# A two-layer hybrid decoder trunk: the order of instructions made by the scheduler's timeline model instead of its default one

## Chip, cores and metric

The kernel runs on one core of a Trainium2 chip. The metric is the device time of one execution in microseconds (us); the median of several runs is compared. A core has five engines with a queue of instructions each: TensorE (PE; its weight loads are listed apart as PEld), VectorE (DVE), ScalarE (ACT), GpSimd (POOL) and SyncE (SP), which issues the loads here.

## The reference

Two layers on one sequence of 512 tokens and 2048 channels, all in float32:

```python
for l in range(DEPTH):                               # 2
    h = rms_norm(x, pre_norm_g[l])
    proj = jnp.einsum('bsd,de->bse', h, w_in[l])     # 2048 -> 6656
    (rq, rk, rv, rg, dq, dk, dv, dg, lx, lg) = jnp.split(proj, split_idx, axis=-1)
    ret_out  = rms_norm(retention(rq, rk, rv, positions)) * silu(rg)             # 6 heads x 128, rope, chunks of 128
    diff_out = rms_norm(diff_attention(dq, dk, dv, positions, lam), subln_g) \
               * (1 - lam_init) * silu(dg)                                       # 4 heads, two softmaxes each, rope, causal
    lru_out  = rg_lru(lx, ...) * silu(lg)                                        # 768 channels, conv of 4, block gates, scan
    y = jnp.einsum('bse,ed->bsd', concat([ret_out, diff_out, lru_out]), w_out[l])
    x = x + rms_norm(y, post_norm_g[l])
```

(The reshapes into heads are left out.)

## The kernel before

Both projections are done in passes. A pass makes 512 output columns: four PSUM banks (`big`, 128 x 512 each, four buffers in all), or two in each of the last two passes of a layer. For each bank it runs over 16 blocks of 128 input rows. Every float32 operand is split into a rounded part and a remainder, so one product is three matmuls (`whi` with `hhi`, `whi` with `hlo`, `wlo` with `hhi`); these are the lines L208. With the output projection the second operand is `mhi`/`mlo`. Form "A" has the weights as the stationary operand (queries, keys, LRU inputs), form "B" the activations (values, gates, output).

Weights come in chunks of two row blocks: SP loads `raw`, ACT rounds it to `whi` (L163), DVE subtracts to get `wlo` (L164). There are three buffers of each (`WBUFS = 3`). The matmuls of one chunk for all banks need its `whi` from the first and its `wlo` from the third on.

The passes of a layer follow in this order: values of the differential attention (`dv`), its queries and keys (`dq`, `dk`), three passes for the LRU (`lx`, `lg`), three for the retention's queries and keys (`rq`, `rk`), three for its values and gates (`rv`, `rg`), the attention's gate (`dg`), then the output projection. When a bank is full it is evacuated: for queries and keys L439 makes `qk` on DVE, and the rope follows: two 64-row products on DVE (L399, L400, output `rt2`), two steps on POOL (L401, L406). For values and gates L535, L738, L740 and L742 read the bank.

Between the matmuls of the passes lies the side work, written as generators that are advanced one step for every two bank groups (`pump`): the attention by blocks of 128 queries and heads, the LRU in two halves, the retention by heads, and the norms. One attention unit makes two score tiles `sc` on PE (L462, L463), adds the mask and takes the row maximum `mx` on DVE (L465, L468), exponentiates to `pr` on ACT (L471), combines the two on DVE (L475 to L477), transposes to `wT` on PE (L485, copied by L487), and multiplies by the values into `acc` (L495). The tiles `sc`, `wT` and `hT` share three PSUM buffers (`pm`). A retention head makes `rs` (L661), `rk` (L665), `kv` and `ro` (L686, L689) on PE; its norm is L692 on ACT, L694 and L695 on DVE, L697 on POOL, L698 and L700 on DVE. At the end of a layer's output passes each bank gives `y` (L767 to L797), and `hT` (L805) transposes it for the next layer, where L812 on ACT and L813 on DVE make `hhi` and `hlo` of it in turn. In the output projection the attention's output is transposed by L552 to `dT` and split by L554 (ACT, `mhi`) and L555 (DVE, `mlo`).

The program's text is not the order in which the engines run. The tile framework collects the instructions and orders those of PE, DVE, ACT and POOL itself, among what the data and the buffers allow, and puts in the semaphores; loads and splits of weights and the evacuation of a full bank are given a higher priority in the text. Only SP keeps the order as written:

```python
    ctx.enter_context(tc.manual_schedule(engines={mybir.EngineType.SP}))
...
        for n, (c, b) in enumerate(order):
            ensure(base + max(c, n // nb) + 2)
            mm(c, b)
            if n % 2 == 1:
                pump()
```

Each engine then runs its instructions strictly in that order. In what follows a name such as `wlo_699` is a tile with the number that the program gives it, which is the same before and after; the profile's rows leave the numbers out.

## Time and profile before

| | |
|---|---|
| median of 3 runs | 1665.82 us (1663.75 to 1666.63) |
| the profiled execution | 1666.37 us, span 1664.4 us, mean granted clock 0.993 |
| PE busy | 1634.2 us, 98% of the span |
| DVE, ACT, POOL busy | 928.7, 626.0, 259.1 us |
| HBM read, written | 167.86 MB, 8.39 MB |

The profile is one execution. The span runs from the first to the last instruction. A row of the timeline gives start, length, engine, line, operation, out<-in and, in brackets, how long the engine had been idle before it and what it waited for. A group row gives the count, busy us and mean ns of one, then the idle time before the group and what ended it. The recorded 0.39 us of a matmul overlaps the next one's, so its price is read from the distance of starts. A half clock of TensorE shows as a granted clock near 0.50 in a stretch.

### The profile page before, as it was taken

To read this page: it belongs to the slowest core of one execution; us is meant where nothing else is said; L and a number is where in the kernel's file an instruction comes from. 1 tells how busy PE (TensorE), PEld (TensorE's weight loads), DVE (VectorE), ACT (ScalarE), POOL (GpSimd) and SP (SyncE) were. 2 spreads that over 40 slices of the span, in tenths; PEclk is the share of its full clock that TensorE was granted. 3 is DMA by queue.
4 is the path that set the end of the run, shared out by engine and by line. 5 is a ranking of instruction groups with operands and counts; after the bars stand their busy time and mean duration, and the time that the engine had idled before them with its cause. 6 is when DMAs were issued, how large, how long until landed. Compare 5 with 4: busy or idle time off the path is not lost. (4 is left out here: it accounts for less than half of the span.)

```text
span 1664.4 us, 19440 instructions
## 1 busy us (share of the span) xinstructions
PE 1634.2 (98%) x7541; PEld 1349.5 (81%) x7541; DVE 928.7 (56%) x1474; ACT 626.0 (38%) x966; POOL 259.1 (16%) x216
## 2 busy tenths in 40 slices
PE   9999899999999999999999998999999999999997
PEld 7788788787877888888888887888888888888886
DVE  6767765665674444322772776664677544442336
ACT  6232345457212323222662224346541222332233
POOL 0011400111261110000110131003035301100003
PEclk9999999999999999999999999999999999999999
DMA  7233222232322222344643222222323322223635
GB/s 258 79 92 101 89 64 84 89 96 76 102 76 77 76 89 83 107 146 158 222 159 100 89 89 77 76 84 83 92 86 102 101 73 77 91 96 108 196 124 199
DMA packets 54747, 177.50 MB, mean 107 GB/s; under 512 B 6656, under 2 KB 7680, under 8 KB 54656
## 3 DMA queue, kind: packets, MB, share of 16 engines
q1 hardware_dynamic: 52592, 169.94, 32.2%
q0 software_dynamic: 1920, 6.29, 1.0%
q8 instruction: 59, 0.97, 0.2%
q14 instruction: 32, 0.26, 0.1%
q10 hardware_dynamic: 144, 0.04, 0.0%
HBM read 167.86 MB, written 8.39 MB: 106 GB/s over the span
## 5 line engine op out<-in xcount | busy, mean ns | idle before, releaser
L164 DVE TENSOR_TENSOR wlo<-raw,whi 128x1024 fp32r<-128x1024 f32 (+1 forms) x289 | 370.5, 1286 | 426.7 <-ACT whi L163 412.8
L163 ACT CAST whi<-raw 128x1024 fp32r<-128x1024 f32 (+1 forms) x289 | 302.6, 1049 | 630.2 <-PE big L208 549.1
L208 PE MATMUL big<-hhi,whi 128*128 128x512 f32 x1024 | 402.9, 394 | 1.5 <-DVE lx L635 1.5
L208 PE MATMUL big<-hhi,wlo 128*128 128x512 f32 x1024 | 400.6, 391 | 1.6 <-DVE wlo L164 1.6
L208 PE MATMUL big<-hlo,whi 128*128 128x512 f32 x1024 | 400.0, 391 | 0.0
L208 PE MATMUL big<-whi,hhi 128*128 128x512 f32 x640 | 255.3, 401 | 3.7 <-ACT rv L738 2.6
L208 PE MATMUL big<-wlo,hhi 128*128 128x512 f32 x640 | 252.0, 395 | 2.7 <-DVE wlo L164 2.7
L208 PE MATMUL big<-whi,hlo 128*128 128x512 f32 x640 | 251.6, 393 | 0.0
L208 PEld LDWEIGHTS big<-hhi,wlo 128*128 128x128 f32 x1024 | 192.9, 188 | 42.5 <-DVE wlo L164 2.0
L208 PEld LDWEIGHTS big<-hhi,whi 128*128 128x128 f32 x1024 | 193.0, 188 | 41.7 <-DVE lx L635 2.0
L208 PEld LDWEIGHTS big<-hlo,whi 128*128 128x128 f32 x1024 | 193.0, 189 | 38.8
L208 PE MATMUL big<-wlo,mhi 128*128 128x512 f32 x512 | 199.5, 390 | 0.6 <-DVE wlo L164 0.6
L208 PE MATMUL big<-whi,mlo 128*128 128x512 f32 x512 | 199.8, 390 | 0.0
L208 PE MATMUL big<-whi,mhi 128*128 128x512 f32 x512 | 199.8, 390 | 0.0
L208 PEld LDWEIGHTS big<-wlo,hhi 128*128 128x128 f32 x640 | 121.5, 190 | 29.4 <-DVE wlo L164 3.1
L208 PEld LDWEIGHTS big<-whi,hhi 128*128 128x128 f32 x640 | 121.5, 190 | 28.3 <-ACT rv L738 3.0
L208 PEld LDWEIGHTS big<-whi,hlo 128*128 128x128 f32 x640 | 121.6, 190 | 24.2
L208 PEld LDWEIGHTS big<-wlo,mhi 128*128 128x128 f32 x512 | 96.1, 188 | 21.2 <-DVE wlo L164 1.5
L208 PEld LDWEIGHTS big<-whi,mlo 128*128 128x128 f32 x512 | 96.2, 188 | 19.7
L208 PEld LDWEIGHTS big<-whi,mhi 128*128 128x128 f32 x512 | 96.1, 188 | 19.6
L773 POOL TENSOR_TENSOR ry<-sy,mhalf 128x1 f32<-128x1 f32 x8 | 4.7, 585 | 406.7 <-DVE sy L771 406.7
L471 ACT ACTIVATE pr<-sc,mx 128x128 f32<-128x128 f32 (+3 forms) x64 | 33.3, 525 | 75.7 <-DVE mx L468 75.6
(212 smaller groups left out, 1530.0 us busy)
## 6 DMA issues: line engine op xcount, KB each, us to landing
raw<-in_w_in SPq DMA_DIRECT2D x207, 512.0 KB, 3.6
raw<-in_w_out SPq DMA_DIRECT2D x80, 512.0 KB, 3.5
xT<-in_xt SPq DMA_DIRECT2D x16, 256.0 KB, 6.6
xr<-in_x SPq DMA_DIRECT2D x16, 256.0 KB, 5.5
xs<-y POOLq DMA_DIRECT2D x16, 256.0 KB, 3.5
xr<-xs SPq DMA_DIRECT2D x16, 256.0 KB, 5.5
pg<-in_postg SPq DMA_DIRECT2D x8, 256.0 KB, 3.9
out<-y POOLq DMA_DIRECT2D x8, 256.0 KB, 4.5
```

Of the source, the lines that this page charges most:

```text
L163: last_copy[0] = A.copy(hi[:, a:b, :], raw[:, a:b, :])
L164: V.tensor_tensor(lo[:, a:b, :], raw[:, a:b, :], hi[:, a:b, :], op=ALU.subtract)
L208: T.matmul(ps[b], lhsT=lhsT, rhs=rhs, start=(cnt[b] == 0), stop=(cnt[b] == total - 1))
L471: A.activation(p[:, :n], sc[c][:, :n], AF.Exp, bias=mx[:, c:c + 1], scale=0.125, accum_out=sums[:, h:h + 1])
L773: G.tensor_tensor(st["ry"][tb], ms, mhalf[:, :1], op=ALU.pow)
```

## The change

One argument is added where the kernel is built:

```diff
-    with tile.TileContext(nc) as tc:
+    with tile.TileContext(nc, schedule_with_timeline_sim=True) as tc:
         tile_hybrid_trunk(tc, *args)
```

With it the framework orders PE, DVE, ACT and POOL by a model of when each instruction would run, instead of its default one. The instructions stay the same, except that ACT's activation tables are loaded 27 times instead of 32. SP's order is the same. Three places show how the rows move.

VectorE, keys of the retention in layer 1 (`qk_692` is the last bank of a pass, `wlo_699` the remainder of the next weights, `rt2` the rope halves). The difference between the two orders, first the head of the block, then its end:

```order
 L164 TENSOR_TENSOR wlo_686_3601<-raw_684_3599,whi_685_3600 128x1024
 L439 TENSOR_TENSOR qk_692_3663<-big_647_3363,rsb_99_457 128x512
-L164 TENSOR_TENSOR wlo_699_3671<-raw_697_3669,whi_698_3670 128x1024
 L399 TENSOR_TENSOR rt2_700_3687<-qk_573_2984,sin_r_92 64x512
 L400 TENSOR_TENSOR rt2_700_3687<-qk_573_2984,sin_r_92 64x512
```

```order
 L399 TENSOR_TENSOR rt2_720_3862<-qk_687_3611,sin_r_92 64x512
 L400 TENSOR_TENSOR rt2_720_3862<-qk_687_3611,sin_r_92 64x512
+L164 TENSOR_TENSOR wlo_699_3671<-raw_697_3669,whi_698_3670 128x1024
+L164 TENSOR_TENSOR wlo_703_3706<-raw_701_3704,whi_702_3705 128x1024
 L164 TENSOR_TENSOR wlo_707_3741<-raw_705_3739,whi_706_3740 128x1024
 L164 TENSOR_TENSOR wlo_711_3776<-raw_709_3774,whi_710_3775 128x1024
```

`wlo_699` has moved from just behind `qk_692` to behind all twelve rope halves, and `wlo_703` from among them to just after it.

TensorE, attention of layer 1, from one unit's scores (`sc_375`) on. Before:

```order
L208 MATMUL big_269_1591<-hhi_51_217,wlo_340_1840 128x512
L462 MATMUL sc_375_1995<-st_241_1430,st_205_1188 128x384
L463 MATMUL sc_375_1995<-kl_243_1436,st_205_1188 128x384
L462 MATMUL sc_376_1998<-st_242_1431,st_206_1189 128x384
L463 MATMUL sc_376_1998<-kl_244_1437,st_206_1189 128x384
L485 MATMUL wT_380_2012<-cmt_81,pr_366_1949 128x128 x3
L495 MATMUL acc_349_1879<-dv_109_513,wT_370_1960 128x128
L495 MATMUL acc_349_1879<-dv_110_527,wT_370_1960 128x128
L208 MATMUL big_270_1592<-hhi_48_211,whi_339_1839 128x512
L208 MATMUL big_270_1592<-hlo_49_212,whi_339_1839 128x512
L208 MATMUL big_270_1592<-hhi_48_211,wlo_340_1840 128x512
L208 MATMUL big_270_1592<-hhi_51_217,whi_339_1839 128x512
```

Now:

```order
L462 MATMUL sc_375_1995<-st_241_1430,st_205_1188 128x384
L463 MATMUL sc_375_1995<-kl_243_1436,st_205_1188 128x384
L462 MATMUL sc_376_1998<-st_242_1431,st_206_1189 128x384
L463 MATMUL sc_376_1998<-kl_244_1437,st_206_1189 128x384
L495 MATMUL acc_349_1879<-dv_109_513,wT_370_1960 128x128
L495 MATMUL acc_349_1879<-dv_110_527,wT_370_1960 128x128
L485 MATMUL wT_380_2012<-cmt_81,pr_366_1949 128x128 x3
L462 MATMUL sc_396_2075<-st_249_1491,st_211_1243 128x384
L463 MATMUL sc_396_2075<-kl_251_1497,st_211_1243 128x384
L462 MATMUL sc_397_2078<-st_250_1492,st_212_1244 128x384
L463 MATMUL sc_397_2078<-kl_252_1498,st_212_1244 128x384
L208 MATMUL big_417_2177<-hhi_7_129,whi_389_2049 128x512
```

The big matmuls that stood between the scores and transposes of the units are now ahead of them all; the first big matmul of the next pass (`big_417`) comes right after the third unit's scores (`sc_396`, `sc_397`).

TensorE, retention of layer 2, behind the last output product of head `ro_1861`. Before:

```order
L686 MATMUL ro_1861_10398<-rv_1799_10026,sT_1854_10356 128x128
L689 MATMUL ro_1861_10398<-rst_1860_10382,qk_1665_9154 128x128
L208 MATMUL big_1800_10076<-whi_1845_10300,hhi_1117_6209 128x512
L208 MATMUL big_1800_10076<-whi_1845_10300,hlo_1118_6210 128x512
L208 MATMUL big_1800_10076<-wlo_1846_10301,hhi_1117_6209 128x512
```

Now:

```order
L686 MATMUL ro_1861_10398<-rv_1799_10026,sT_1854_10356 128x128
L689 MATMUL ro_1861_10398<-rst_1860_10382,qk_1665_9154 128x128
L661 MATMUL rs_1887_10526<-qk_1710_9431,qk_1760_9766 128x128 x2
L665 MATMUL rk_1888_10531<-cmt_81,qk_1760_9766 128x128 x3
L208 MATMUL big_1880_10504<-whi_1867_10417,hhi_1087_6095 128x512
L208 MATMUL big_1880_10504<-whi_1867_10417,hlo_1088_6096 128x512
L208 MATMUL big_1880_10504<-wlo_1868_10418,hhi_1087_6095 128x512
```

The new bank `big_1880` takes the buffer of `big_1800`; where the matmuls of `big_1800` to `big_1803` followed the head's output, the next head's `rs` and `rk` and the new bank now do.

## Prediction

> **What bounds the kernel now.** I read the head of the profile page first, then the chain that ended last, then TensorE's waits, then the timeline around the longest waits, and last a table of stretches with the clock.

> ```profile
> span 1664.4 us, 19440 instructions
> PE 1634.2 (98%) x7541; PEld 1349.5 (81%) x7541; DVE 928.7 (56%) x1474; ACT 626.0 (38%) x966; POOL 259.1 (16%) x216
> ```

> TensorE is the bound: 98% busy, while VectorE, the next, stands at 56%. The chain view (start, length, what) gives the price of one matmul:

> ```profile
> 1483.09 147.82 PE big L208 x652
> ```

> 147.82 / 652 = 0.2267 us. The kernel has 6528 of these 128x512 matmuls (17 passes of 16 x 4 x 3 in each of two layers; the diff leaves the count alone), so 1480 us are theirs whatever the order, and the small matmuls of the three mixers fill nearly all the rest. An order can only change how long TensorE stands still. That is the view of waits (total us, times, longest), the larger rows:

> ```profile
> PE sc L462 <- ACT pr L471: 5.2, 3, 2.8
> PE big L208 <- DVE wlo L164: 4.9, 4, 2.7
> PE big L208 <- ACT rv L738: 2.6, 1, 2.6
> PE big L208 <- DVE lx L635: 1.5, 1, 1.5
> PE ssx L915 <- DVE xsq L907: 1.4, 1, 1.4
> PE big L208 <- ACT whi L163: 1.1, 1, 1.1
> ```

> These are 16.7 us; the smaller rows (all under 1 us each, without the start's) bring it to about 20. Four of them in the timeline, with the wait in brackets:

> ```profile
> 199.59 0.33 PE L462 MATMUL sc<-st,st 128*128 128x128 f32 x1 [1.73 <-ACT pr L471]
> 475.59 0.50 PE L208 MATMUL big<-wlo,hhi 128*128 128x512 f32 x1 [2.70 <-DVE wlo L164]
> 505.46 0.50 PE L208 MATMUL big<-whi,hhi 128*128 128x512 f32 x1 [2.59 <-ACT rv L738]
> 1005.05 0.39 PE L462 MATMUL sc<-st,st 128*128 128x128 f32 x1 [2.80 <-ACT pr L471]
> ```

> and behind the three longest, and behind the one at 48.8 us (ssx), the clock is halved. Columns: stretch, its length, busy time of PE, PEld, DVE, ACT, POOL, then granted clock, DMA share, GB/s:

> ```profile
> 49.40:56.30 6.90, 6.90 (x25) 5.79 (x26) 2.17 (x9) 1.29 (x2) 1.03 (x1) 0.51 0.01 2
> 476.10:479.50 3.40, 3.40 (x9) 2.63 (x9) 3.40 (x2) 0.00 (x0) 2.71 (x2) 0.50 0.66 182
> 506.80:510.20 3.40, 3.40 (x10) 2.63 (x9) 1.23 (x1) 1.04 (x1) 0.00 (x0) 0.51 0.28 104
> 1005.20:1012.00 6.80, 6.12 (x17) 4.80 (x18) 3.14 (x12) 2.05 (x8) 0.00 (x0) 0.50 0.43 142
> ```

> A stretch costs half its length: 3.4 + 1.7 + 1.7 + 3.4 = 10.2 us. The wait of 1.73 at 199.6 brought none.

> **What the change removes.** In the new order I followed each waiting instruction back to what it waits for: nearly every wait above has its producer earlier or its reader later. For instance the last weights (wlo) are now read some 14 matmuls before the end, not 24. So 20 us of waits go, 10.2 us of half clock, and 0.1 us at each of about 20 restarts: 32 us. What is late instead are the places below; the rest of the order moves work that keeps its lead, and I set it at nothing because each reader stands at least as many matmuls behind its producer as the producer's chain takes. Where that cover is too short it is in the list.

> **E, retention's keys in layer 1.** VectorE now runs twelve rope halves (L399, L400) between qk_692 and wlo_699; before, wlo_699 came first. In the same place of the trace (rows of VectorE, then groups in the stretch 453.5 to 473.5):

> ```profile
> 445.28 0.69 DVE L439 TENSOR_TENSOR qk<-big,rsb 128x512 f32<-128x512 f32 x1 [0.61 <-PE big L208]
> 448.00 0.69 DVE L439 TENSOR_TENSOR qk<-big,rsb 128x512 f32<-128x512 f32 x1 [2.03 <-PE big L208]
> 451.36 0.69 DVE L439 TENSOR_TENSOR qk<-big,rsb 128x512 f32<-128x512 f32 x1
> L400 DVE TENSOR_TENSOR rt<-qk,sin_r 64x512 f32<-64x512 f32 x6 | 9.1, 1516 | 0.1
> L399 DVE TENSOR_TENSOR rt<-qk,sin_r 64x512 f32<-64x512 f32 x6 | 8.0, 1340 | 0.2
> L164 DVE TENSOR_TENSOR wlo<-raw,whi 128x1024 fp32r<-128x1024 f32 x3 | 6.1, 2028 | 0.1
> ```

> The banks come 2.72 us apart (12 matmuls), so the third, qk_692's, was complete near 450.7. The new order has 56 matmuls from there to the first reader of wlo_699: 56 x 0.2267 = 12.7, so it is wanted at 463.4. VectorE has it at 452.05 + 17.1 + 0.3 of gaps + about 2.0 = 471.4. TensorE stands 8.0 us; such a wait is past any that the trace shows, so I take the longer half-clock stretch, 3.3. **11.3.** From below the ends are 0 (see the rival on ropes), from above 14.

> **RQ and RK, the same in layer 2.** Ten ropes stand ahead of wlo_1733, whose reader comes 74 matmuls (16.8 us) after the last bank; eight stand ahead of wlo_1769 (54 matmuls, 12.2 us). Groups of the stretch 1239.8 to 1255.2:

> ```profile
> L400 DVE TENSOR_TENSOR rt<-qk,sin_r 64x512 f32<-64x512 f32 x5 | 7.4, 1484 | 0.1
> L399 DVE TENSOR_TENSOR rt<-qk,sin_r 64x512 f32<-64x512 f32 x5 | 5.4, 1078 | 0.1
> ```

> Ten are 12.8 us, behind two splits of the mixer rows (1.3) that stay where they were; with 2 us for wlo_1733 it ends 1.5 us late. Eight, at E's means, are 11.4; with wlo 13.4 after qk_1762, whose 0.7 lies past its bank: 2.0 late, 0.5 for clock. **1.5 + 2.5.**

> **C, D: differential attention.** One unit is two score products, a mask and maximum each (L465), L468, two exponentials (L471), the combination (L477), transposes. Groups by line and shape, mean ns in the second number:

> ```profile
> L465 DVE CUSTOM_DVE_ANT_0 sc<-sc,cmt 128x384 f32<-128x384 f32 x16 | 8.7, 572 | 1.8 <-PE sc L463 1.8
> L465 DVE DVE_READ_ACCUMULATOR2_ANT mx<- 128x1 f32 x64 | 9.0, 140 | 0.0
> L471 ACT ACTIVATE pr<-sc,mx 128x384 f32<-128x384 f32 x16 | 9.2, 578 | 22.7 <-DVE mx L468 22.6
> L471 ACT ACTIVATION_READ_ACCUMULATOR pr<-sc,mx 128x1 f32 x64 | 12.5, 196 | 0.0
> L477 DVE SCALAR_TENSOR_TENSOR pr<-pr,cc,pr 128x384 f32<-128x384 f32 x8 | 5.6, 704 | 0.2
> L812 ACT ACTIVATE hhi<-hT,pp 128x128 fp32r<-128x128 f32 x64 | 20.5, 370 | 6.3 <-DVE hlo L813 5.1 <-PE hT L805 1.0
> L813 DVE SCALAR_TENSOR_TENSOR hlo<-hT,pp,hhi 128x128 fp32r<-128x128 f32 x64 | 19.6, 345 | 2.7 <-ACT hhi L812 2.4
> ```

> At C (layer 1, the end of a pass) three units now follow each other on TensorE with no big matmul between. From the scores of sc_365 to pr_366, which wT_380 reads: two L465 1.42, the weight split wlo_423 queued among them 1.3, L468, L475, L476 some 0.5, two exponentials 1.55, the next unit's L465 0.71, L477 0.70: 6.2 us, and a second split (wlo_393) up to 1.3 ahead of it. TensorE has 1.3 us of its own there. 6.1 and 1.7 of clock: **7.8** (2 to 9). At D (layer 2) the same happens once, with wlo_1530 between L465 and L468 of the unit whose pr_1484 is next: waits 3.1, clock 1.7, some 0.2 at the place of the old 2.80: **5.0** (2 to 6).

> **H, layer boundary.** Four hT transposes (1116, 1125, 1158, 1159) now stand in a row with three PSUM buffers for them. One buffer is free after four L812 and four L813 that follow each other by turns: about 4 x 0.37 + 0.35 = 1.8 us, while the post-norm's VectorE work lies between them. Walked by hand: 4.15 us in several waits, and 1.7 of clock: **5.8** (1.5 to 7.5).

> **J, retention in layer 2.** big_1880 now stands directly behind ro_1861, rs_1887 and rk_1888, some 1.0 us of work. It needs the bank of big_1800, which is read by the silu, value and gate instructions queued behind ro_1861's normalisation:

> ```profile
> 1370.18 0.60 ACT L692 ACTIVATE rsq<-ro 128x512 f32<-128x512 f32 x1 [0.74 <-PE ro L689]
> 1370.80 1.28 ACT L535 ACT_TABLE_LOAD   x1
> 1374.61 0.61 DVE L742 SCALAR_TENSOR_TENSOR rg<-big,rstd,rgs 128x128 f32<-128x128 f32 x2 [0.44 <-ACT rv L738]
> ```

> From 1370.1 to 1375.2 are 5.1 us; less 1.0 it waits 4.1, and 1.7 of clock: **5.8** (3 to 7.5). Five of the 32 table loads (1.28 each) vanish from ACT, none of them here; ACT has idle time around them, so I give nothing for that.

> **G, output projection, both layers.** dT_931 and dT_1997 move to just ahead of the first matmul that reads whi_940 (whi_2006). ACT makes that weight after dT's evacuation:

> ```profile
> 663.36 0.69 ACT L554 ACTIVATE mhi<-dT,subg 128x512 fp32r<-128x512 f32 x1 [0.48 <-PE dT L552]
> 663.95 1.04 ACT L163 CAST whi<-raw 128x1024 fp32r<-128x1024 f32 x1
> ```

> 0.69 + 1.04 = 1.7 us in each layer, 3.5, with 0.5 for clock: **4.0** (3.4 to 7). **I**, the LRU gate of layer 1 waiting behind POOL: **1** (0 to 2.5).

> **K, the end.** The last two banks now end 4 matmuls (0.9 us) apart, not 18 (4.1):

> ```profile
> 1655.12 0.39 PE L208 MATMUL big<-wlo,mhi 128*128 128x512 f32 x1
> 1655.60 0.60 ACT L767 ACTIVATE junk<-big 128x512 f32<-128x512 f32 x1 [1.86 <-PE big L208]
> 1657.14 3.08 DVE L797 SCALAR_TENSOR_TENSOR y<-y,ry,xr 128x512 f32<-128x512 f32 x3
> ```

> VectorE's part for a bank is 4 us (three L797, 3.08, and what leads to them). Before, the first bank's ran beside TensorE; now about 3 us of it come between the last matmul and the last outputs: **3** (1 to 4).

> **Sum.** 11.3 + 4.0 + 7.8 + 5.0 + 5.8 + 5.8 + 4.0 + 1 + 3 = 47.7 lost, 32 won: +15.7 on the profiled execution, whose time is 1666.37 (2.0 outside its span). The median of the runs is 0.5 lower, so I say 1681.

> [...] The rows above put the half clock behind waits of 2.6 to 2.8 us. [...]

> **Rivals.** No change: the rope halves at E, RQ and RK take 0.69 us, as some single ones do in the trace, not the mean of 1.4, because POOL's part of the rope falls elsewhere. Then wlo_699 is ready at 452.05 + 8.3 + 1.3 = 461.7, ahead of 463.4, and all three terms go: -15.3, so 1666. For it: RQ's five L399 have a mean of 1078 ns and E's six 1340, so the slow-down depends on what runs beside them. Against: POOL does its part of a rope as soon as these same rope halves let it, so it runs beside the next ones. Faster: every wait of the new order stays below 1.9 us, as most of the old did, so that no half clock follows. Ten places at 1.9 are 19 us against 32: -13, so 1653. It decides from 3 us for a place downwards. For it: only three old waits behind attention and weights were longer; against it: the queues at E, C and J hold 5 to 17 us in rows. Much slower: each of six long waits (C, D, E, H, J, RK) is followed by 6.8 us of half clock, as at 1005, which is up to 10 us more: 1691.

> **How the numbers follow.** My forecast has 0.54, much slower 0.14, no change 0.13, faster 0.19. A change under 0.2% (3.3 us) can't be told from none. Slower 0.68, same 0.13, faster 0.19. The range goes from 1661, below which lies more than half of the faster case, to 1693, above which I leave 0.05; the likeliest case alone has 1673 to 1689.

> **What would show it.** TensorE's waits should show wlo (L164) as the largest releaser, with one of about 8 us near 465 to 475; three waits around sc or wT near 235 to 245 us; one of 4 us behind rg (L742) in the second layer's retention; whi (L163) at both output projections; half clock behind each wait over 2.5 us; and none at 49, 506 and 1005. I am wrong if the waits of TensorE sum to under 25 us, or if VectorE's ropes at E are short.

## The result, and the profile after

The changed kernel takes 1681.28 us (median of 4 runs, 1679.88 to 1683.64) against 1665.38 us for the kernel before on the same chip (1663.75 to 1666.63): a ratio of 1.0097, 95% interval 1.0080 to 1.0115, so 15.9 us slower. The profiled execution took 1679.92 us, 13.6 us more than that of before, with a span of 1678.1 us.

The head of the page after:

```profile
span 1678.1 us, 19433 instructions
PE 1632.7 (97%) x7541; PEld 1350.2 (80%) x7541; DVE 937.0 (56%) x1474; ACT 618.9 (37%) x961; POOL 264.0 (16%) x216
```

TensorE's busy time is 1.5 us less than before and its span 13.7 us more. It does the same work and stands still longer. Its waits by releaser (total us, times, longest), without two rows of 1.4 us (at the start) and 1.2 us:

```profile
PE big L208 <- DVE wlo L164: 13.1, 5, 7.7
PE sc L462 <- ACT pr L471: 5.0, 3, 2.4
PE big L208 <- ACT rgs L535: 4.4, 1, 4.4
PE big L208 <- ACT whi L163: 3.5, 2, 1.8
PE big L208 <- DVE qk L439: 2.5, 1, 2.5
PE hT L805 <- DVE hlo L813: 1.8, 2, 1.5
```

Before, the last weights (`wlo`) were the second entry with 4.9 us; now they are the first with 13.1. The waits of over 1 us one by one, in the timeline, wait in brackets:

```profile
174.81 0.50 PE L208 MATMUL big<-hhi,wlo 128*128 128x512 f32 x1 [1.39 <-DVE wlo L164]
238.31 0.69 PE L462 MATMUL sc<-st,st 128*128 128x384 f32 x1 [2.39 <-ACT pr L471]
307.15 0.50 PE L208 MATMUL big<-hhi,whi 128*128 128x512 f32 x1 [1.23 <-DVE lg L640]
355.35 0.50 PE L208 MATMUL big<-hhi,whi 128*128 128x512 f32 x1 [2.54 <-DVE qk L439]
468.10 0.80 PE L208 MATMUL big<-wlo,hhi 128*128 128x512 f32 x1 [7.70 <-DVE wlo L164]
671.12 0.50 PE L208 MATMUL big<-whi,mhi 128*128 128x512 f32 x1 [1.77 <-ACT whi L163]
849.27 0.66 PE L805 MATMUL hT<-cmt,y 128*128 128x128 f32 x4 [1.49 <-DVE hlo L813]
1083.02 0.50 PE L462 MATMUL sc<-st,st 128*128 128x512 f32 x1 [2.09 <-ACT pr L471]
1252.58 0.50 PE L208 MATMUL big<-hhi,wlo 128*128 128x512 f32 x1 [1.28 <-DVE wlo L164]
1294.30 0.50 PE L208 MATMUL big<-wlo,hhi 128*128 128x512 f32 x1 [2.41 <-DVE wlo L164]
1389.31 0.76 PE L208 MATMUL big<-whi,hhi 128*128 128x512 f32 x1 [4.44 <-ACT rgs L535]
1502.65 0.50 PE L208 MATMUL big<-whi,mhi 128*128 128x512 f32 x1 [1.77 <-ACT whi L163]
```

Only the rows at 174.8 and 355.4 are not in the prediction's list. Stretches of the trace with the granted clock (the third number from the end), first at the three old places near 49, 506 and 1005 us, then at the new ones:

```profile
48.00:56.00 8.00, 8.00 (x38) 6.40 (x37) 5.25 (x12) 4.30 (x6) 0.00 (x0) 1.00 0.20 67
500.00:512.00 12.00, 12.00 (x60) 10.08 (x59) 7.83 (x11) 5.24 (x10) 6.86 (x5) 1.00 0.28 87
1005.00:1012.00 7.00, 7.00 (x34) 5.78 (x33) 4.27 (x15) 3.76 (x11) 0.00 (x0) 1.00 0.52 152
238.00:241.40 3.40, 3.09 (x11) 2.65 (x11) 2.39 (x9) 1.26 (x6) 0.00 (x0) 0.52 0.52 167
463.30:473.50 10.20, 5.40 (x13) 4.25 (x14) 9.10 (x6) 0.00 (x0) 9.90 (x5) 0.51 0.32 101
1084.40:1087.80 3.40, 3.40 (x10) 2.62 (x9) 3.30 (x13) 0.31 (x2) 1.01 (x1) 0.50 0.64 202
1388.20:1395.00 6.80, 5.69 (x14) 4.46 (x15) 3.61 (x12) 2.78 (x8) 2.51 (x2) 0.50 0.02 8
```

The old half-clock stretches are gone, and C, E, D and J of the prediction have one each. (Both kernels have one more behind the last matmul, from 1660.5 us before and from 1671.5 us now, where TensorE has nothing left to do.) Where part of a stretch lies inside the wait it costs nothing: at E TensorE works again from 468.1, so (473.4 - 468.1) / 2 = 2.65 us are lost.

### The profile page after: what moved, and what is told of

Read it like the earlier page. It is cut to its first block, busy times and chain, and to the rows that moved or that the text cites. A ratio compares the mean times of both kernels' runs of the same rounds, so it can differ in the third digit from the quotient of the medians.

```text
span 1678.1 us, 19433 instructions
## 1 busy us (share of the span) xinstructions
PE 1632.7 (97%) x7541; PEld 1350.2 (80%) x7541; DVE 937.0 (56%) x1474; ACT 618.9 (37%) x961; POOL 264.0 (16%) x216
## 4 chain that ended last, share of the span: by engine, by line
PE 90%; DVE 6%; ACT 2%; issue 1%; POOL 0%; DVEq 0%; ACTq 0%; POOLq 0%
PE big L208 82%; DVE wlo L164 1%; PE gate L599 1%; PE acc L495 1%; DVE rt L404 1%; PE ro L686 1%; DVE rt L400 1%; PE rs L661 1%; PE sc L462 1%; PE sc L463 1%; PE ro L689 0%; PE kv L675 0%; PE wT L485 0%; ACT whi L163 0%; PE hT L805 0%
## 5 line engine op out<-in xcount | busy, mean ns | idle before, releaser
L164 DVE TENSOR_TENSOR wlo<-raw,whi 128x1024 fp32r<-128x1024 f32 (+1 forms) x289 | 368.9, 1281 | 428.5 <-ACT whi L163 412.6
L163 ACT CAST whi<-raw 128x1024 fp32r<-128x1024 f32 (+1 forms) x289 | 302.2, 1049 | 614.3 <-PE big L208 530.6
L208 PE MATMUL big<-hhi,whi 128*128 128x512 f32 x1024 | 401.5, 392 | 3.8 <-DVE qk L439 2.5
L208 PE MATMUL big<-hlo,whi 128*128 128x512 f32 x1024 | 400.6, 391 | 0.0
L208 PE MATMUL big<-hhi,wlo 128*128 128x512 f32 x1024 | 394.9, 391 | 3.1 <-DVE wlo L164 3.0
L208 PE MATMUL big<-wlo,hhi 128*128 128x512 f32 x640 | 247.9, 396 | 10.1 <-DVE wlo L164 10.1
L208 PE MATMUL big<-whi,hhi 128*128 128x512 f32 x640 | 251.0, 399 | 4.5 <-ACT rgs L535 4.4
L208 PE MATMUL big<-whi,hlo 128*128 128x512 f32 x640 | 251.2, 394 | 0.0
L208 PEld LDWEIGHTS big<-hhi,wlo 128*128 128x128 f32 x1024 | 192.7, 188 | 45.1 <-DVE wlo L164 4.8
L208 PEld LDWEIGHTS big<-hhi,whi 128*128 128x128 f32 x1024 | 192.7, 188 | 44.9 <-DVE qk L439 3.0
L208 PEld LDWEIGHTS big<-hlo,whi 128*128 128x128 f32 x1024 | 192.7, 188 | 39.2
L208 PE MATMUL big<-whi,mhi 128*128 128x512 f32 x512 | 200.2, 391 | 3.5 <-ACT whi L163 3.5
L208 PE MATMUL big<-whi,mlo 128*128 128x512 f32 x512 | 199.4, 390 | 0.0
L208 PE MATMUL big<-wlo,mhi 128*128 128x512 f32 x512 | 192.1, 389 | 0.0
L208 PEld LDWEIGHTS big<-wlo,hhi 128*128 128x128 f32 x640 | 121.6, 190 | 36.6 <-DVE wlo L164 11.2
L208 PEld LDWEIGHTS big<-whi,hhi 128*128 128x128 f32 x640 | 121.4, 190 | 30.2 <-ACT rgs L535 4.7
L208 PEld LDWEIGHTS big<-whi,hlo 128*128 128x128 f32 x640 | 121.4, 190 | 24.5 <-DVE hlo L813 0.3
L208 PEld LDWEIGHTS big<-whi,mhi 128*128 128x128 f32 x512 | 96.1, 188 | 23.6 <-ACT whi L163 4.0
L208 PEld LDWEIGHTS big<-wlo,mhi 128*128 128x128 f32 x512 | 96.0, 188 | 19.9
L208 PEld LDWEIGHTS big<-whi,mlo 128*128 128x128 f32 x512 | 96.1, 188 | 19.7
L471 ACT ACTIVATE pr<-sc,mx 128x128 f32<-128x128 f32 (+3 forms) x64 | 33.2, 524 | 81.1 <-DVE mx L468 81.1
```

Source lines behind the costliest of these rows:

```text
L163: last_copy[0] = A.copy(hi[:, a:b, :], raw[:, a:b, :])
L164: V.tensor_tensor(lo[:, a:b, :], raw[:, a:b, :], hi[:, a:b, :], op=ALU.subtract)
L208: T.matmul(ps[b], lhsT=lhsT, rhs=rhs, start=(cnt[b] == 0), stop=(cnt[b] == total - 1))
L471: A.activation(p[:, :n], sc[c][:, :n], AF.Exp, bias=mx[:, c:c + 1], scale=0.125, accum_out=sums[:, h:h + 1])
```

## The experiments

The theory: a few places in the new order each put one instruction behind work that outlasts its reader's cover, each costs what its wait and the clock behind it cost, and the costs add. The general rival: the order as a whole sets the time, and a place undone turns up as a wait somewhere else. All edits set the order of issue alone, within one engine's queue; only `pool_late` makes one engine wait for another (with `Sync` in place of `NoSync`). They stand behind the call that writes the program, in this form, and in the diffs below only the pairs are shown (an instruction, the one that it must now follow, and a comment with the tiles):

```diff
         tile_hybrid_trunk(tc, *args)
+        ins = {i.name: i for i in nc.cur_bb.bb.instructions}
+        for later, earlier in (
...
+        ):
+            tc.add_manual_dep(ins[later], earlier, mybir.DependencyInfo(
+                mybir.DependencyClass.NoSync, mybir.DependencyReason.DATA), reason="order")
```

**e_only: place E put back, in the changed kernel.**

```diff
+            ("I-3688", "I-3674"),  # DVE: rope halves rt2_700 behind wlo_699
+            ("I-3689", "I-3674"),  # DVE: rope halves rt2_700 behind wlo_699
+            ("I-3828", "I-3709"),  # DVE: rope halves rt2_716 behind wlo_703
+            ("I-3829", "I-3709"),  # DVE: rope halves rt2_716 behind wlo_703
+            ("I-3863", "I-3744"),  # DVE: rope halves rt2_720 behind wlo_707
+            ("I-3864", "I-3744"),  # DVE: rope halves rt2_720 behind wlo_707
```

> The new order with one place put back: on VectorE wlo_699 stands ahead of the twelve rope halves again, wlo_703 behind eight of them and wlo_707 behind ten; all else as in the new order. Theory (the place in the queue makes the wait): the wait of 7.7 us at wlo_699 and the half clock behind it go, together 10.5 us by the trace after, and no other wait comes: 1681.3 - 10.5 = about 1671. Rival (backlog: VectorE has the same work before the same readers, so the wait only moves to wlo_703 or wlo_707, as before the change, when 2.7 us and 1.7 us of half clock stood there): 1675 or more, with a wait of 2 to 4 us within 10 us of the old one.

Measured: 1672.87 us (1672.67 to 1672.94), ratio 1.0048 (1.0033 to 1.0063), 8.4 us off the changed kernel. The waits behind `wlo`:

```profile
PE big L208 <- DVE wlo L164: 5.4, 4, 2.4
```

7.7 of the 13.1 us are gone, and no other entry grew by more than 0.7. So half of the net loss comes from one place on one engine. The gain is 2 us less than expected. Outside E and ahead of the last matmul the clock was halved for 20.5 us in this profile and for 13.7 in the changed kernel's, and half of the difference, 3.4 us, is lost time; the last section has what was measured of that.

**before_e: the same place, the other way, in the kernel before.**

```diff
+            ("I-3674", "I-3864"),  # DVE: wlo_699 behind the last rope half, rt2_720
+            ("I-3674", "I-3863"),  # DVE: and its first part
```

> The kernel before with this one place of the change made alone: wlo_699 (and with it wlo_703) behind all twelve rope halves on VectorE; nothing else moves. Theory: the first reader of wlo_699 stands 50 matmuls behind the bank, so it is wanted at about 462.0 us and ready at 471.5: a wait of 9 us or a little more, with some 2.5 us of half clock behind it, while the old wait of 2.7 us for wlo_707 and its 1.7 us of half clock vanish, since TensorE then comes later: +7, 1672 to 1674. Rival (the wait is TensorE's standing cost there in any order): within 2 us of 1665.4. If the two costs add instead of replacing each other: 1677.

Measured: 1672.42 us (1671.01 to 1674.04), ratio 1.0042 (1.0026 to 1.0059), +7.4. Its timeline and the stretch of half clock around it:

```profile
473.94 0.79 PE L208 MATMUL big<-wlo,hhi 128*128 128x512 f32 x1 [10.94 <-DVE wlo L164]
```

```profile
466.40:480.10 13.70, 6.16 (x15) 4.81 (x16) 11.83 (x7) 0.00 (x0) 10.61 (x6) 0.50 0.26 86
```

The wait of 2.70 at 475.6, which the kernel before had there, is gone. So the place in VectorE's queue is enough to make the wait, without anything else of the new order. (POOL works here too, for 10.61 us of this stretch; the next run is about that.)

**pool_late: are the ropes long because POOL works beside them?** POOL's first step of seven ropes (L401) waits until VectorE has done the last rope half; VectorE's order stays that of the changed kernel.

```diff
+            ("I-3649", "I-3864"),  # POOL: L401 of qk_571 behind the last rope half on VectorE, L400 rt2_720
+            ("I-3690", "I-3864"),  # POOL: L401 of qk_573 likewise
...
+            ("I-3865", "I-3864"),  # POOL: L401 of qk_687 likewise
```

> The new order, wlo_699 still behind the twelve rope halves, but POOL's first rope steps (L401) of these ropes wait until VectorE has done the last half. Theory (the size of the wait is VectorE running beside POOL): each rope half takes 0.69 us instead of the 1.4 on the mean, the twelve take 8.4 instead of 16.7 us, wlo_699 is ready 8 us earlier, near the time it is wanted: the wait falls from 7.7 to under 1 us and the time to about 1671. Rival (rope halves are slow for another reason, such as the weight splits' or ScalarE's traffic): the halves stay at 1.4 us and the time at 1681.

Measured: 1671.85 us (1670.81 to 1673.23), ratio 1.0042 (1.0027 to 1.0057), 9.4 us off the changed kernel. VectorE's groups at E, first of the changed kernel (449 to 466 us), then of this one (446 to 473 us; count, busy us, mean ns):

```profile
L400 DVE TENSOR_TENSOR rt<-qk,sin_r 64x512 f32<-64x512 f32 x6 | 10.1, 1676 | 0.1
L399 DVE TENSOR_TENSOR rt<-qk,sin_r 64x512 f32<-64x512 f32 x6 | 6.4, 1073 | 0.2
```

```profile
L400 DVE TENSOR_TENSOR rt<-qk,sin_r 64x512 f32<-64x512 f32 x7 | 4.8, 686 | 0.1
L399 DVE TENSOR_TENSOR rt<-qk,sin_r 64x512 f32<-64x512 f32 x7 | 4.8, 686 | 0.1
```

With POOL idle (29.1 us ahead of its L401) each rope half takes 0.686 us, where the means are 1.676 and 1.073 us with POOL at work beside them (14.9 of the 17 us), and the 7.7 us wait goes although `wlo_699` still stands behind all twelve. So two things make E together: the place in the queue, and POOL's work beside it. Either one taken away takes the wait. The prediction's rival "no change" had the right mechanism but not its condition. What in POOL's work lengthens a rope half was not shown.

**j_only, g_only, k_only: three more places put back, each alone.**

```diff
+            ("I-10474", "I-10405"),  # PE: big_1802 from whi_1857 on behind the last product of ro_1861
+            ("I-10486", "I-10405"),  # PE: big_1803 from whi_1845 on likewise
+            ("I-10468", "I-10381"),  # PE: big_1802 from whi_1845 on behind kv_1859
+            ("I-10432", "I-10441"),  # ACT: whi_1870 behind rgs_1872
+            ("I-10433", "I-10449"),  # DVE: wlo_1871 behind rg_1876
+            ("I-10512", "I-10445"),  # ACT: whi_1885 behind rv_1874
```

> The new order with the retention place of layer 2 put back: 18 matmuls of big_1802 and big_1803 stand behind ro_1861 again and cover its normalisation, and ScalarE and VectorE round the next weights behind the evacuation of big_1800. Theory: the chain of 5.1 us behind ro_1861 is covered by 4.1 us of matmuls and some 0.5 us of small ones, so the wait of 4.6 us at big_1880 falls to 0.5 to 1 and its half clock (2.5 us of loss) goes: -6.5, about 1675. Rival (the bank's release is set by something else, such as the table load or the next weights): the wait stays above 3 us and the time above 1679.

Measured: 1676.80 us (1675.25 to 1678.43), ratio 1.0072 (1.0057 to 1.0087), 4.5 us won, 2 us less than expected; this profile has half clock at H and RK, where the changed kernel's has none. What is left of the wait of 4.44 at the first matmul of `big_1880`:

```profile
1390.42 0.47 PE L208 MATMUL big<-whi,hhi 128*128 128x512 f32 x1 [0.76 <-DVE rg L742]
```

```diff
+            ("I-5162", "I-5103"),  # PE: big_937, big_938 from whi_916 on behind dT_931
+            ("I-5168", "I-5103"),  # PE: big_937, big_938 from whi_916 on behind dT_931
+            ("I-11264", "I-11205"),  # PE: big_2003, big_2004 from whi_1982 on behind dT_1997
+            ("I-11270", "I-11205"),  # PE: big_2003, big_2004 from whi_1982 on behind dT_1997
```

> The new order with dT_931 and dT_1997 moved twelve big matmuls ahead of the first reader of whi_940 and whi_2006 (as before the change they stood 30 ahead). Theory: the evacuation and the rounding behind dT (0.69 + 1.04 us) run beside these twelve (2.7 us), both waits of 1.8 us go, and nothing else changes: 1681.3 - 3.9 = 1677.4. Rival (the weights come late from memory or from their three buffers, whatever stands on ScalarE ahead of them): the waits stay and the time is within 1 us of 1681.

Measured: 1676.24 us (1675.12 to 1679.10), ratio 1.0070 (1.0056 to 1.0084), 5.0 us won, 1.1 more than expected and within the runs' spread; both waits behind `whi` (3.5 us) are gone from the view.

```diff
+            ("I-12340", "I-12323"),  # PE: big_2153 from whi_2164 on behind the last matmul of big_2152
+            ("I-12346", "I-12323"),  # PE: from whi_2167 on
+            ("I-12352", "I-12323"),  # PE: from whi_2170 on
```

> The new order with the last eighteen matmuls of big_2153 put behind big_2152's last one again. Theory: VectorE's 4 us for the first of the two banks run beside these matmuls again, so from the last matmul's start to the end of VectorE's work are 5.1 us instead of 8.0; the two waits for the last weights (0.4 and 0.2 us, of 0.6 and 0.4 between matmuls) come back: the tail is 2.9 us shorter and the time 2 us. Rival (the tail is set by the stores): the tail stays at 8 us.

Measured: one execution, 1681.12 us. The tail alone answers: from the start of the last matmul to the end of VectorE's last row it is 1674.92 - 1669.81 = 5.1 us, as in the kernel before, against 8.0 in the changed one. The total says nothing, since this execution had more half clock ahead of its last matmul (six stretches, 30.7 us, against four, 23.9 us, in the changed kernel's profile), so K's price in the total was not settled alone.

**before_a: the start's gain, tried with one engine.** The new order has no half clock at 49 us. First guess: because VectorE's sums of squares (L907) come ahead of two weight splits. The edit is in the kernel before.

```diff
+            ("I-464", "I-397"),  # DVE: wlo_102 behind the last sum of squares (L907)
+            ("I-494", "I-397"),  # DVE: wlo_105 likewise
```

> The kernel before with one gain of the change made alone: at the start VectorE adds up the squares (L907) ahead of the weight remainders wlo_102 and wlo_105, for which it otherwise waits 3.6 us on ScalarE. Theory: the sums are ready 5 us earlier, the wait of 1.4 us at ssx goes and with it the 6.8 us of half clock behind it (3.4 us lost): 1665.2 - 5 = 1660. Rival (the half clock at 49 us comes from the small matmuls of ssx and not from the wait): only the wait goes, 1663.7, with a clock of 0.5 still behind ssx.

Measured: 1664.94 us (10 runs, 1660.38 to 1669.02), ratio 1.0002 (0.9991 to 1.0012): a miss. Three rows of its timeline, ScalarE's, VectorE's and TensorE's:

```profile
38.97 1.05 ACT L163 CAST whi<-raw 128x1024 fp32r<-128x1024 f32 x1 [3.86 <-PE big L208]
40.58 0.69 DVE L907 TENSOR_TENSOR xsq<-xsq,xsq 128x512 f32<-128x512 f32 x1 [4.75 <-ACT xsq L905]
48.52 3.25 PE L915 MATMUL ssx<-ones,xsq 128*128 128x1 f32 x16 [2.12 <-DVE xsq L907]
```

VectorE was ready and waited for ScalarE's squares; these stood behind ScalarE's own weight roundings, which waited for TensorE. In the changed kernel ScalarE does all 16 squares in one go at 25.4 us:

```profile
25.38 8.43 ACT L905 ACTIVATE xsq<-xT 128x512 f32<-128x512 f32 x16
```

**before_a2: the same with both engines.**

```diff
+            ("I-463", "I-396"),  # ACT: whi_101 behind the last square (L905)
+            ("I-493", "I-396"),  # ACT: whi_104 likewise
+            ("I-464", "I-397"),  # DVE: wlo_102 behind the last sum of squares (L907)
+            ("I-494", "I-397"),  # DVE: wlo_105 likewise
```

> Before with the whole start of the new order: ScalarE's rounding of the weights whi_101 and whi_104 stands behind its last square (L905), and VectorE's wlo_102 and wlo_105 behind its last sum of squares (L907); all else in the order of before. Theory (the start's gain is the order of both engines together; moving VectorE alone left VectorE waiting for ScalarE's squares): TensorE's wait at ssx goes, and with it the 6.8 us of half clock at 49 us, about 5 us in all: 1660. Rival 1 (the weights that now come later are wanted soon after, and the wait moves to the first matmuls that read whi_101): 1665, no change, with a new wait on whi between 55 and 70 us. Rival 2 (the loads from HBM set the start in both orders): 1665, with the ssx wait still there.

Measured: 1660.52 us (9 runs, 1656.68 to 1662.60), ratio 0.9971 (0.9961 to 0.9980), 4.3 us under the kernel before. The stretch at the start:

```profile
40.00:60.00 20.00, 20.00 (x99) 16.61 (x98) 12.38 (x25) 6.29 (x8) 1.03 (x1) 1.00 0.31 98
```

No wait and full clock where the kernel before has 6.8 us of half clock. So this part of the gain is the move of ScalarE's squares and VectorE's sums together. VectorE's move does nothing alone; ScalarE's alone was not tried.

**repaired: all places that could be put back, together.** E, RQ, RK, J and G, K with 12 matmuls in place of 18, and one more: the wait at 174.8, `kl_243` and `kl_244` behind `wlo_247`. 26 pairs of the kind above, among them:

```diff
+            ("I-9693", "I-9574"),  # DVE: rt2_1750 behind wlo_1737
...
+            ("I-9950", "I-9831"),  # DVE: rt2_1786 behind wlo_1773
...
+            ("I-12346", "I-12323"),  # PE: big_2153 from whi_2167 on behind the last of big_2152
...
+            ("I-1440", "I-1459"),  # DVE: kl_243 (L432) behind wlo_247
```

> The new order with seven places put right by local constraints: the rope blocks of both layers (E, RQ, RK), retention in layer 2 (J), both output projections (G), the end (twelve matmuls of big_2153 behind big_2152) and one wait for wlo_247 that both orders have (1.6 us). Theory (the places are independent and their costs add): 10.5 + 1.4 + 2.6 + 4.5 + 3.9 + 2.2 + 1.6 = 26.7 off 1681.3 = 1654.6, below both kernels, with some 14 us of waits left (attention twice, the layer boundary, the LRU). Rival (costs do not add: a wait that is taken away lets TensorE run into the next one): 1662 or more, with waits that neither profile has.

Measured: 1653.77 us (5 runs, 1651.31 to 1654.46), ratio 0.9926 (0.9913 to 0.9940): 27.5 us under the changed kernel and 11.2 under the kernel before. The costs add, to within 2.2 us, which is the size of one run's own interval: from the three runs alone E 8.4, J 4.5 and G 5.0, and from the trace RQ and RK 4.0, K with 12 matmuls 1.8 (its tail is 6.2 us, not 8.0) and the wait at 174.8 1.6, together 25.3.

**repaired_D, repaired_H: two places more,** each added alone to the repaired kernel: the scores of D behind big matmuls, and big matmuls between the transposes of H again.

```diff
+            ("I-8306", "I-8467"),  # PE: sc_1503 behind twelve matmuls of big_1524
+            ("I-8367", "I-8473"),  # PE: sc_1515 behind twelve of big_1525
```

```diff
+            ("I-6586", "I-6231"),  # PE: big_1167 from whi_1171 on behind hT_1125
+            ("I-6411", "I-6591"),  # PE: hT_1158 behind big_1167
+            ("I-6426", "I-6599"),  # PE: hT_1159 behind six matmuls of big_1168
```

> The repaired kernel (1653.8) with place D repaired too: in layer 2's attention sc_1503 stands behind 12 matmuls of big_1524 and sc_1515 behind 12 of big_1525. Theory (the wait there is units following each other without cover): 2.3 us of waiting and 1.7 of half clock go, 1650. Rival (big matmuls moved there are missed where they came from): 1653.8 or more, with a new wait on sc, wT or big within 30 us of the place.

> The repaired kernel (1653.8) with place H repaired too: at the layer boundary the transposes hT_1125, hT_1158 and hT_1159 have big matmuls of big_1167 and big_1168 between them again. Theory: the waits of hT and big there (2.4 us in after's profile, three pieces, none followed by half clock in that profile) go: 1651.4. Rival (what they wait for is the post-norm's VectorE work, which is not sooner done): the same sum of waits at other matmuls, 1653.8.

Measured: 1654.17 us (1652.40 to 1655.24), ratio 0.9934 (0.9921 to 0.9948), and 1655.23 us (1651.39 to 1655.97), ratio 0.9943 (0.9928 to 0.9958). Neither gains; the rival was right at both. D in the repaired kernel, then in repaired_D:

```profile
1071.71 0.53 PE L462 MATMUL sc<-st,st 128*128 128x512 f32 x1 [2.08 <-ACT pr L471]
```

```profile
1072.07 0.79 PE L208 MATMUL big<-hhi,whi 128*128 128x512 f32 x1 [2.46 <-DVE lx L635]
```

The scores no longer wait, but the next big matmul does, at the same time, for the bank that VectorE empties (L635). H in repaired_H:

```profile
831.94 0.66 PE L805 MATMUL hT<-cmt,y 128*128 128x128 f32 x4 [1.47 <-DVE hlo L813]
835.30 0.47 PE L208 MATMUL big<-whi,hhi 128*128 128x512 f32 x1 [0.88 <-DVE y L774]
836.32 0.50 PE L208 MATMUL big<-whi,hlo 128*128 128x512 f32 x1 [0.55 <-DVE hlo L813]
838.16 0.50 PE L208 MATMUL big<-whi,hlo 128*128 128x512 f32 x1 [0.88 <-DVE hlo L813]
```

3.8 us in four pieces where the repaired kernel has 1.8 in two. At both places the wait goes on to another matmul that needs VectorE, so it looks to be VectorE's work that is late there, whichever reader comes first. That is only argued: the pairs name TensorE's instructions alone, and another order on VectorE was not tried, nor were repairs of C and of the wait at 355.

## Why the prediction was right, and where not

It said 1681.0 us, slower; measured are 1681.28. The places and the mechanism held. The sum held partly because errors of both signs cancel, so that it came within 0.3 us is luck. Its terms against the changed kernel's profile (a wait here is the distance of matmul starts less the usual one, some 0.2 us over the bracket, more where small waits follow; the clock is half of the stretch that lies behind the wait):

| place | predicted, wait + clock | profile, wait + clock | its own run |
|---|---|---|---|
| E | 8.0 + 3.3 | 8.2 + 2.7 | 8.4 (e_only) |
| RQ, RK | 3.5 + 0.5 | 4.0 + 0 | |
| C | 6.1 + 1.7 | 3.7 + 1.5 | |
| D | 3.3 + 1.7 | 2.3 + 1.7 | |
| H | 4.15 + 1.7 | 2.4 + 0 | |
| J | 4.1 + 1.7 | 4.9 + 2.9 | 4.5 (j_only) |
| G | 3.5 + 0.5 | 3.9 + 0 | 5.0 (g_only) |
| I | 1 | 1.4 | |
| K | 3 | 2.9 | tail 2.9 (k_only) |
| not foreseen (355) | 0 | 3.2 + 0 | |
| sum | 47.7 | 45.7 | |

- **The gain.** 32 us were said. 45.7 less the 13.6 that the profiled pair differs by is 32.1, by subtraction; with the 15.9 between the medians it is 29.8. Only the start's part of it was tried by itself (before_a2). The old half-clock stretches at 49, 506 and 1005 are gone, as said; one wait that I counted as won is not: the one behind `wlo_247` at 174.8 stayed (1.6 us).
- **E** is shown from both sides (e_only, before_e), and with its second condition (pool_late). The twelve ropes took 16.5 us where 17.1 were said, and the wait came within 0.2 us. Neither sign of being wrong showed: TensorE's waits sum to 31.5 us without the start's, over the 25 named, and the ropes were not short.
- **RQ's 1.5 does not follow from its terms.** 0.7 for the evacuation, 1.3, 12.8 and 2 make 16.8 us, just the cover of 74 matmuls; with the 0.66 us that lay ahead of the evacuation at E and 0.3 of gaps it is 1.0 late. The trace has 1.28 us (the row at 1252.58), so the nearness is partly luck.
- **C is the term that was mis-sized most in its wait: 3.7 against 6.1.** I followed the chain from the scores to the combination (L477) that `wT_380` reads. In the trace TensorE waits earlier and for less: the row at 238.31 is a score tile that waits for the exponential (L471) to free a buffer, so the combination is not what TensorE stood for. D is the same step with the same error, 2.3 against 3.3. "Three waits around sc or wT" were two of weight.
- **H: 2.4 against 4.15, and no half clock, so with its clock (5.8 said) the term that was furthest off.** My walk by hand put the post-norm's VectorE work in series with the splits; the trace has waits of 1.49, 0.34 and 0.11 us.
- **J came larger, and the releaser is another.** I named L742 on VectorE; it is ScalarE's gate (L535), as these rows of ScalarE show:

```profile
1384.75 1.28 ACT L535 ACT_TABLE_LOAD   x1
1386.04 0.47 ACT L535 ACTIVATE rgs<-big,rstd 128x256 f32<-128x256 f32 x1
1388.15 0.37 ACT L738 ACTIVATE rv<-big,rstd 128x128 f32<-128x128 f32 x1 [1.64 <-DVE rv L740]
1388.42 1.20 ACT L535 ACTIVATE rgs<-big,rstd 128x256 f32<-128x256 f32 x3
```

  The last three gates stand behind a value copy that waits 1.64 us for VectorE. I had counted the table load, not the turn between the two engines.
- **The wait at 355 was missed.** I set "the rest of the order" at nothing because each reader has as many matmuls of cover as its producer's chain takes. At 355 that chain is longer than I counted. VectorE's rows:

```profile
352.27 1.18 DVE L627 TENSOR_TENSOR gt<-gt,gt 128x512 f32<-128x512 f32 x1 [3.02 <-ACT gt L626]
353.48 1.23 DVE L629 TENSOR_TENSOR_SCAN lh<-la,gt 128x512 f32<-128x512 f32 x1
354.62 0.67 DVE L439 TENSOR_TENSOR qk<-big,rsb 128x512 f32<-128x512 f32 x1
```

  The evacuation that TensorE needs (L439) stands behind the LRU's scan, which stands behind a product that waits 3.02 us for ScalarE. By these rows it is place E again with another instruction behind the batch; no run put it back.
- **The clock terms** came to 8.8 us against 11.1 in this profile. "Half clock behind each wait over 2.5 us" is wrong: 2.39 and 2.09 us had one, 2.41 and 2.54 had none. A row of before stood against it already: the 6.8 us of half clock at 49 us follow a wait of 1.4 us (ssx). My bound by length does not fit these waits; the last section has what fits, as far as it goes.
- **Of the rivals,** "faster" needed waits below 1.9 us at ten places; six of the new waits were longer. "Much slower" needed 6.8 us of half clock behind six waits; J has 6.8 and E 10.2, the others 3.4 or none.

## What to carry to other kernels

When an order of instructions changes, look at each engine for an urgent instruction (a weight split, an evacuation) that now stands behind a batch whose head waits for a third engine, and set the batch's time, measured beside what runs with it, against the matmuls left before the reader. Here such places were few, the costs of those put back added up, and the gains elsewhere were kept: 26 pairs turned a loss of 15.9 us into a gain of 11.2. Where a repair on one engine only hands the wait to the next reader, as at D and H, look at the engine that does the late work, not at the one that waits.

## What the runs showed of the hardware

**Equal waits had a half clock behind them in one profile and none in another.** The same wait of 2.41 us at RK stands in the changed kernel's profile (the row at 1294.30) and in that of e_only, and so does H's of 1.49 (the row at 849.27). The rows of e_only:

```profile
840.73 1.11 PE L805 MATMUL hT<-cmt,y 128*128 128x128 f32 x4 [1.49 <-DVE hlo L813]
1286.56 0.50 PE L208 MATMUL big<-wlo,hhi 128*128 128x512 f32 x1 [2.41 <-DVE wlo L164]
```

and the stretches behind them, first in the changed kernel (with the one behind the 2.54 us at 355), then in e_only:

```profile
355.40:358.80 3.40, 3.06 (x12) 2.21 (x13) 3.40 (x5) 0.52 (x2) 0.00 (x0) 1.00 0.00 0
849.30:852.70 3.40, 3.31 (x14) 2.11 (x14) 3.40 (x9) 2.06 (x8) 0.54 (x1) 1.00 0.00 0
1294.00:1297.50 3.50, 3.20 (x14) 2.63 (x15) 3.46 (x3) 0.00 (x0) 3.08 (x2) 1.00 0.43 150
```

```profile
840.70:844.10 3.40, 3.37 (x10) 2.88 (x11) 3.40 (x8) 1.97 (x8) 0.54 (x1) 0.50 0.00 0
1287.80:1291.20 3.40, 3.40 (x9) 2.65 (x9) 3.35 (x4) 0.00 (x0) 2.77 (x2) 0.50 0.36 137
```
